# Storing the split halves of weight tiles in DRAM, in a two-layer hybrid trunk

## The chip, the cores and the metric

The kernel runs on one core of one Trainium2 chip. The metric is the device time of one execution in microseconds (us). A core has TensorE (PE in the profile; its weight loads are PEld), VectorE (DVE), ScalarE (ACT), GpSimd (POOL) and SyncE (SP), which here issues all DMAs between the chip's DRAM and the on-chip memory (SBUF). SyncE's queue is kept in order: an issue that waits for a semaphore holds up all issues behind it.

## What is computed

The reference is one inference step of a two-layer trunk: a prompt of 2048 rows of 1024 channels, and eight decode rows with states of their own. Each layer is

```python
hn = rms_norm(x, norm_w)
proj = hn @ w_in                    # 1024 x 3332
# split into four head groups, each with a mixer of its own:
#   A RetNet retention, H HGRN2 recurrence, S S5 state space + GLU, M Mamba-2 SSD
mixed = concatenate([o_ret, o_hgrn, o_s5, o_m2], axis=-1)
x = x + mixed @ w_out               # 1024 x 1024
```

The four mixers are recurrences along the prompt, and the states at its end are outputs too. A final RMSNorm ends the trunk.

## The kernel before

**Blocks and stages.** The prompt is cut into 4 blocks of 512 rows, so two layers make 8 blocks. A block has the input projections `gemm_A`, `gemm_H`, `gemm_S`, `gemm_M`, the mixers `mix_A` to `mix_M` and the output projection `out_proj`. A written order (`ORDER`) interleaves them: the S5 mixing of a block and its output projection run in the middle of the next block's phases. The decode rows ride along with the first block of each layer (`B.dec`).

**Split weights.** The products keep nearly full fp32 accuracy by splitting each operand into a high half, rounded to the fast type `float32r`, and the rest. A product is then three TensorE passes: low x high, high x low, high x high (`for pi, (a, c) in enumerate(((1, 0), (0, 1), (0, 0)))`). The activations are split once per block. The weights are loaded and split again for every block, tile by tile: SyncE loads 256 KB into a `wr` tile (`raw`), ScalarE casts it into the high half of a `wh` tile (`hl`; L606, L642), and VectorE subtracts that from the raw tile into the low half (L607, L643). The products of the decode rows use the raw tile, in the first block of a layer alone.

**Tiles.** `gemm_wide` takes 512 columns by 128 rows of the weight (L641 loads, L647 multiplies), `gemm` 256 columns by 2 x 128 rows (L603 loads, L605 the 4 tail columns of the time step; L622 and L590 multiply). A block has 68 tiles either way: 36 with `gemm` and 32 with `gemm_wide` in the first block of layer 0, 28 and 40 in the others, and in the last block the output projection goes by `gemm`, which makes 44 and 24.

**Buffers and order.** There are 7 buffers for `wr` (`NWR`) and 6 for `wh` (`NWH`). A `wr` buffer is free after the subtract (in a layer's first block, after the decode product); a `wh` buffer after the tile's last product on TensorE. The load, cast and subtract of a tile are traced with a raised priority (`WPRI` = 100); a planner orders each engine's instructions by priority and by its own idea of when operands and buffers are ready. [...]

**Other transfers.** The rows of a block are read twice (`xn`, 512 KB each: L526, L560), the residual in the output projection (L1538) is read and `xmid` written (L1543), and the S5 mixing reads seven constant tables of 512 KB (`big<-s5c`, L248). L1258 stores the S5 input into a tile of another layout, L752 writes decode rows, L1501 loads the final norm's weights.

Of the kernel before, what the change touches and what calls it, by code (L numbers as in the profile page):

```python
# [20 lines left out]
P = 128  # L21
D = 1024
KT = 8
# [93 lines left out]
def trunk_kernel(ctx: ExitStack, tc: tile.TileContext, A: dict):  # L117
# [31 lines left out]
    def nm(s):  # L149
        uid[0] += 1  # L150
        return f"{s}_{uid[0]}"
# [92 lines left out]
    s5c = [[drp.tile([P, 1024], F32, name=f"s5c{i}_{j}", tag=f"s5c{i}_{j}") for j in range(7)] for i in range(DEPTH)]  # L244

# [330 lines left out]
    def gemm(lhs, w, c0, mode, evac, dec=None, tail=None, ks=(0, 1, 2, 3), late=False):  # L576
# [55 lines left out]
    def gemm_wide(lhs, w, c0, evac, dec=None):  # L632
# [398 lines left out]
    def gemm_A(L, B):  # L1031
        w = A["w_in"][L.l]
# [14 lines left out]
        if B.l == 0 and B.b == 0:  # L1047
            qks = {}
            for part in range(2):
# [7 lines left out]
                gemm(B.hn, w, C_RQ + 256 * part, "T", ev1, dec=dec, late=part == 0)  # L1057
            B.qk = lambda tt, i: qks[i // 2, tt // 2][:, (tt % 2) * 256 + (i % 2) * P : (tt % 2) * 256 + (i % 2) * P + P]
        else:
# [7 lines left out]
            gemm_wide(B.hn, w, C_RQ, ev1, dec=dec)  # L1067
# [7 lines left out]
        gemm_wide(B.hn, w, C_RV, ev2, dec=B.dec and B.dec.chunk("rv"))  # L1075
# [53 lines left out]
    def gemm_H(L, B):  # L1129
        w = A["w_in"][L.l]  # L1130
# [11 lines left out]
        gemm(B.hn, w, C_GQ + 256, "F", ev1, dec=dec)  # L1142
        gemm(B.hn, w, C_GQ, "F", lambda m, ps: S.activation(B.gq[:, m, :], ps, AF.Silu), dec=dec)
# [7 lines left out]
        gemm_wide(B.hn, w, C_GI, ev2, dec=dec)  # L1151
# [98 lines left out]
    def gemm_S(L, B):  # L1250
        w = A["w_in"][L.l]
# [525 lines left out]
```

## Time and profile before

| | |
|---|---|
| time before | 2353.92 us, median of 3 runs (2349.15 to 2357.65) |
| span of the profiled execution | 2351.3 us |
| TensorE busy | 2186.8 us, 93% |
| VectorE busy | 1690.8 us, 72% |
| ScalarE busy | 1007.4 us, 43% |
| GpSimd busy | 247.0 us, 11% |
| DMA | 283.89 MB, mean 121 GB/s |
| mean granted clock of TensorE | 0.973 of full speed |

The profile is of one execution. Its span runs from the first to the last instruction; its time as a run was not listed apart from the three runs, and the span lies inside their spread. Busy shares are means over stages of different kind. TensorE's products are pipelined and their ends are modelled, so back-to-back products take less than their mean duration. Names such as `gb<-wh,hn` are the tile written and the tiles read; `wh` and `wr` are the split and raw weight tiles, `gb` the accumulators of the projections, `mb` those of everything else, `hn` and `mx` the split activations.

### The profile page before, as it was taken

Reading aid. Unit: us, or ns where it says so; the run is one execution under the profiler, and the core shown is the slowest. Engines: PE = TensorE matmul, PEld = TensorE weight load, DVE = VectorE, ACT = ScalarE, POOL = GpSimd, SP = SyncE. Lnnn points to the kernel's source line nnn. Section 1 sums busy time; section 2 is a strip of 40 time slices with the busy share of each in tenths; the row PEclk is TensorE's granted clock in tenths of the full one; section 3 lists DMA queues with packets and bytes.
Section 4 is the critical chain, followed back from the end, with each engine's and each line's share of the span. In section 5 each row is a group of like instructions: output and inputs, shape, how many; then the busy total and the mean of one; then the engine's idle time right before and its main releaser. Section 6 shows DMA issues by size and latency. Waiting matters only on the chain.

```text
span 2351.3 us, 41033 instructions
## 1 busy us (share of the span) xinstructions
PE 2186.8 (93%) x15047; PEld 1724.8 (73%) x15047; DVE 1690.8 (72%) x4625; ACT 1007.4 (43%) x1873; POOL 247.0 (11%) x212
## 2 busy tenths in 40 slices
PE   7997899999989999999899987999999999999897
PEld 6766676686767877788676775776877787777687
DVE  6778885578866687558856588855985568766686
ACT  5334545245442353424534245443454344443543
POOL 1020011001111011001110001100011001100100
PEclk9998899999999999999999998999999999999998
DMA  5334543433434644251333424526244352337222
GB/s 190 89 95 103 159 154 76 129 107 118 133 101 147 139 126 141 75 167 47 125 126 114 134 65 153 162 46 182 86 153 157 104 175 64 95 122 260 64 65 83
DMA packets 259226, 283.89 MB, mean 121 GB/s; under 512 B 88208, under 2 KB 184608, under 8 KB 259024
## 3 DMA queue, kind: packets, MB, share of 16 engines
q1 hardware_dynamic: 259024, 281.26, 39.8%
q8 instruction: 119, 1.95, 0.3%
q14 instruction: 83, 0.68, 0.1%
HBM read 245.00 MB, written 31.99 MB: 118 GB/s over the span
## 4 chain that ended last, share of the span: by engine, by line
PE 57%; DVE 20%; issue 6%; ACT 3%; DMA 2%; SPq 1%; POOL 1%; ACTq 0%; DVEq 0%; POOLq 0%
PE gb L647 25%; PE gb L622 10%; PE gb L590 5%; DVE big L1191 2%; PE mb L1332 1%; PE mb L1183 1%; DVE wh L643 1%; PE mb L569 1%; DMA big<-s5c 1%; DVE hHb L1240 1%; DVE half L1299 1%; PE gb L652 1%; PE mb L663 1%; SPq L940 1%; PE mb L1198 1%
## 5 line engine op out<-in xcount | busy, mean ns | idle before, releaser
L647 PE MATMUL gb<-wh,hn 128*128 128x512 f32 x2208 | 558.0, 402 | 4.9 <-DVE wh L643 4.3
L622 PE MATMUL gb<-hn,wh 128*128 128x512 f32 x1920 | 491.5, 403 | 0.1
L647 PEld LDWEIGHTS gb<-wh,hn 128*128 128x128 f32 x2208 | 408.1, 190 | 110.3 <-issue 13.5
L622 PEld LDWEIGHTS gb<-hn,wh 128*128 128x128 f32 x1920 | 348.9, 188 | 89.4 <-issue 8.8
L642 ACT CAST wh<-wr 128x512 fp32r<-128x512 f32 x296 | 182.7, 620 | 375.9 <-PE gb L647 184.5
L647 PE MATMUL gb<-wh,mx 128*128 128x512 f32 x1344 | 338.0, 402 | 0.0
L643 DVE TENSOR_TENSOR wh<-wr,wh 128x512 fp32r<-128x512 f32 x296 | 208.6, 712 | 170.5 <-ACT wh L642 169.6
L607 DVE TENSOR_TENSOR wh<-wr,wh 128x512 fp32r<-128x512 f32 (+1 forms) x248 | 176.9, 724 | 169.5 <-ACT wh L606 163.6
L647 PEld LDWEIGHTS gb<-wh,mx 128*128 128x128 f32 x1344 | 247.7, 189 | 63.5 <-issue 6.9
L606 ACT CAST wh<-wr 128x512 fp32r<-128x512 f32 (+1 forms) x248 | 151.6, 621 | 268.1 <-PE gb L647 103.8
L590 PE MATMUL gb<-wh,hn 128*128 128x256 f32 (+1 forms) x1728 | 233.3, 291 | 4.2 <-DVE hn L553 4.1
L590 PEld LDWEIGHTS gb<-wh,hn 128*128 128x128 f32 x1728 | 218.2, 194 | 13.3 <-DVE hn L553 5.9
L1445 POOL TENSOR_TENSOR half<-mats,m_lal 128x512 fp32r<-128x512 f32 x64 | 71.7, 1148 | 511.1 <-DVE m_lal L1423 301.6
L1183 PE MATMUL mb<-zb,big 128*64 128x64 f32 x1536 | 66.5, 242 | 38.8 <-ACT zb L1176 31.5
L1191 DVE COPY_PREDICATED big<-lvl,mb 64x256 f32<-64x256 int32 x192 | 93.0, 537 | 10.3 <-PE mb L1183 6.4
L1176 ACT COPY zb<-big 64x512 f32<-64x512 f32 x112 | 70.3, 628 | 64.0 <-DVE big L1204 54.2
L1183 PEld LDWEIGHTS mb<-zb,big 128*64 128x64 f32 x1536 | 56.6, 152 | 53.5 <-ACT zb L1176 38.2
L1166 POOL TENSOR_TENSOR big<-mats,h_dg 128x1024 f32<-128x1024 f32 x16 | 34.0, 2140 | 557.8 <-DVE h_dg L1163 438.5
L1367 DVE SCALAR_TENSOR_TENSOR big<-gb,vt,big 128x511 f32<-128x511 f32 (+2 forms) x96 | 66.9, 739 | 12.0 <-ACT big L1365 11.8
L671 ACT ACTIVATE half<-mb 128x512 f32<-128x512 f32 x32 | 19.1, 598 | 88.3 <-PE mb L1227 47.8
L1348 DVE TENSOR_TENSOR half<-half,big 128x512 f32<-128x512 f32 x16 | 10.9, 687 | 63.1 <-ACT half L1347 63.1
L1042 POOL TENSOR_TENSOR half<-half,half 128x256 f32<-128x256 f32 x32 | 27.2, 850 | 235.0 <-DVE half L1040 85.2
(493 smaller groups left out, 3240.7 us busy)
## 6 DMA issues: line engine op xcount, KB each, us to landing
wr<-in_w_in SPq DMA_DIRECT2D x416, 256.0 KB
wr<-in_w_out SPq DMA_DIRECT2D x128, 256.0 KB
big<-s5c SPq DMA_DIRECT2D x56, 512.0 KB
xn<-xmid SPq DMA_DIRECT2D x32, 512.0 KB
xn<-in_x_prompt SPq DMA_DIRECT2D x24, 512.0 KB
xmid<-half SPq DMA_DIRECT2D x44, 256.0 KB
half<-xmid SPq DMA_DIRECT2D x44, 256.0 KB
half<-in_x_prompt SPq DMA_DIRECT2D x32, 256.0 KB
```

The source lines that it names most:

```text
L590: T.matmul(out, lhs[2 * ks[ki] + k][:, a, tt * P : (tt + 1) * P], hls[ki][:, c, k, :n], start=(ki == 0 and k == 0 and pi == 0 and tt % per ...
L606: S.copy(hl[:, 0, :, :n], raw[:, :, :n])
L607: V.tensor_tensor(hl[:, 1, :, :n], raw[:, :, :n], hl[:, 0, :, :n].bitcast(F32), ALU.subtract)
L622: T.matmul(banks[i], hl[:, a, k, i * P : (i + 1) * P], lhs[2 * k2 + k][:, c, :], start=(ki == 0 and k == 0 and pi == 0), stop=(ki == 3 and ...
L642: S.copy(hl[:, 0, 0:512], raw[:, 0:512])
L643: V.tensor_tensor(hl[:, 1, 0:512], raw[:, 0:512], hl[:, 0, 0:512].bitcast(F32), ALU.subtract)
L647: T.matmul(banks[tt], lhs[kt][:, a, tt * P : (tt + 1) * P], hl[:, c, 0:512], start=(kt == 0 and pi == 0), stop=(kt == KT - 1 and pi == 2))
L1176: S.copy(qz[sl, r, :].rearrange("p (b h) -> p b h", h=h), q[sl].rearrange("p a (b two h) -> p (a b) two h", two=2, h=h)[:, :, 1, :])
L1183: T.matmul(ps[su, j * 64 : (j + 1) * 64], k[:, j // 4, (j % 4) * P + 64 * u : (j % 4) * P + 64 * u + 64], qz[:, :, j * 64 + 32 * u : j * 6 ...
L1191: V.copy_predicated(stv[p][su, :, nu * u : nu * u + nu, :], mv, ps[su, p * 256 : p * 256 + 256].rearrange("p (c b h) -> p c b h", c=8, h=h))
L1367: V.scalar_tensor_tensor(acc[:, 3 - i :], ps[:, : TB - 3 + i], w(i), acc[:, 3 - i :], ALU.mult, ALU.add)
L1445: E('m').tensor_tensor(mm.rearrange("p (h t) -> p h t", h=4), tri[:, None, :].to_broadcast([P, 4, P]), lal[:, i, tt, :][:, :, None].to_bro ...
```

## The change

The kernel gets a DRAM tensor `wsp` for each layer's `w_in` and `w_out`, with both halves of every element side by side by row. In the first block of a layer (`fresh`) tiles are loaded and split as before, and each split tile is also written to `wsp` by SyncE. In the other three blocks a tile's two halves are loaded straight into the `wh` tile, with no `wr` tile, cast or subtract. `gemm` does this in two DMAs of 256 KB per tile, one for each 128 rows (two more of 4 KB where there are tail columns), and `gemm_wide` in one DMA of 512 KB. Pieces stay 1 KB long in `gemm` and 2 KB in `gemm_wide`. Buffers, priorities and the written order are not touched. Every caller passes `fresh = B.b == 0` and the name of the weight in place of its array.

```diff
+    wsp = {(n, i): drp.tile([KT, P, 2, c], F32, name=f"ws_{n}{i}", tag=f"ws_{n}{i}")
+           for i in range(DEPTH) for n, c in (("w_in", PROJ), ("w_out", D))}
...
-    def gemm(lhs, w, c0, mode, evac, dec=None, tail=None, ks=(0, 1, 2, 3), late=False):
+    def gemm(lhs, wl, c0, mode, evac, dec=None, tail=None, ks=(0, 1, 2, 3), late=False, fresh=False):
+        w, ws = A[wl[0]][wl[1]], wsp[wl]
...
-                raw = wrp.tile([P, 2, 260], F32, name=nm("wr"), tag="wr")
-                rows = w[2 * k2 * P : 2 * (k2 + 1) * P].rearrange("(k p) c -> p k c", p=P)
-                nc.sync.dma_start(raw[:, :, 0:256], rows[:, :, c0 : c0 + 256])
-                if tail is not None:
-                    nc.sync.dma_start(raw[:, :, 256:260], rows[:, :, tail : tail + 4])
-                S.copy(hl[:, 0, :, :n], raw[:, :, :n])
-                V.tensor_tensor(hl[:, 1, :, :n], raw[:, :, :n], hl[:, 0, :, :n].bitcast(F32), ALU.subtract)
+                parts = [(0, 256, c0)] + ([(256, 260, tail)] if tail is not None else [])
+                raw = None
+                if fresh:
+                    raw = wrp.tile([P, 2, 260], F32, name=nm("wr"), tag="wr")
+                    rows = w[2 * k2 * P : 2 * (k2 + 1) * P].rearrange("(k p) c -> p k c", p=P)
+                    for a, b, c in parts:
+                        nc.sync.dma_start(raw[:, :, a:b], rows[:, :, c : c + b - a])
+                    S.copy(hl[:, 0, :, :n], raw[:, :, :n])
+                    V.tensor_tensor(hl[:, 1, :, :n], raw[:, :, :n], hl[:, 0, :, :n].bitcast(F32), ALU.subtract)
+                for k in range(2):
+                    for a, b, c in parts:
+                        d = ws[2 * k2 + k, :, :, c : c + b - a]
+                        if fresh:
+                            nc.sync.dma_start(d, hl[:, :, k, a:b].bitcast(F32))
+                        else:
+                            nc.sync.dma_start(hl[:, :, k, a:b].bitcast(F32), d)
...
-    def gemm_wide(lhs, w, c0, evac, dec=None):
+    def gemm_wide(lhs, wl, c0, evac, dec=None, fresh=False):
+        w, ws = A[wl[0]][wl[1]], wsp[wl]
...
-                raw = wrp.tile([P, 520], F32, name=nm("wr"), tag="wr")
-                nc.sync.dma_start(raw[:, 0:512], w[kt * P : (kt + 1) * P, c0 : c0 + 512])
-                S.copy(hl[:, 0, 0:512], raw[:, 0:512])
-                V.tensor_tensor(hl[:, 1, 0:512], raw[:, 0:512], hl[:, 0, 0:512].bitcast(F32), ALU.subtract)
+                raw = None
+                d = ws[kt, :, :, c0 : c0 + 512]
+                if fresh:
+                    raw = wrp.tile([P, 520], F32, name=nm("wr"), tag="wr")
+                    nc.sync.dma_start(raw[:, 0:512], w[kt * P : (kt + 1) * P, c0 : c0 + 512])
+                    S.copy(hl[:, 0, 0:512], raw[:, 0:512])
+                    V.tensor_tensor(hl[:, 1, 0:512], raw[:, 0:512], hl[:, 0, 0:512].bitcast(F32), ALU.subtract)
+                    nc.sync.dma_start(d, hl[:, :, 0:512].bitcast(F32))
+                else:
+                    nc.sync.dma_start(hl[:, :, 0:512].bitcast(F32), d)
...
-        w = A["w_in"][L.l]
+        w, fresh = ("w_in", L.l), B.b == 0
...
-                gemm_wide(B.mix, w, hf * 512, evac_wide(hf), dec=B.dec and B.dec.out(hf, last))
+                gemm_wide(B.mix, w, hf * 512, evac_wide(hf), dec=B.dec and B.dec.out(hf, last), fresh=fresh)
```

## Rows read from the trace of the kernel before

**Rows 1.** The page: span, busy time by engine, DMA queues.
```profile
span 2351.3 us, 41033 instructions
...
PE 2186.8 (93%) x15047; PEld 1724.8 (73%) x15047; DVE 1690.8 (72%) x4625; ACT 1007.4 (43%) x1873; POOL 247.0 (11%) x212
...
q1 hardware_dynamic: 259024, 281.26, 39.8%
```

**Rows 2.** Groups by line: busy us, mean ns | idle before, what ended it.
```profile
L647 PE MATMUL gb<-wh,hn 128*128 128x512 f32 x2208 | 558.0, 402 | 4.9 <-DVE wh L643 4.3 <-DVE rs L234 0.3
...
L643 DVE TENSOR_TENSOR wh<-wr,wh 128x512 fp32r<-128x512 f32 x296 | 208.6, 712 | 170.5 <-ACT wh L642 169.6
L642 ACT CAST wh<-wr 128x512 fp32r<-128x512 f32 x296 | 182.7, 620 | 375.9 <-PE gb L647 184.5 <-PE gb L622 59.6 <-DMA wr<-in_w_out 47.7
L607 DVE TENSOR_TENSOR wh<-wr,wh 128x512 fp32r<-128x512 f32 (+1 forms) x248 | 176.9, 724 | 169.5 <-ACT wh L606 163.6 <-DMA half<-xmid 2.1 <-DMA wr<-in_w_out 2.1
```

**Rows 3.** Chain of waits, 1600 to 1680 us: start, us, what.
```profile
1625.47 0.96 PE gb L652 x4
1626.43 5.74 PE gb L647 x24
...
1639.81 22.50 PE gb L622 x96
```

**Rows 4.** Waits of TensorE: us in total, times, longest.
```profile
PE mb L1183 <- ACT zb L1176: 31.5, 16, 5.4
```

**Rows 5.** Sum of the six stretches 294:590:870:1150 and 1450:1740:2020:2352 us: busy us.
```profile
sum 1758.00, PE 1664.28 PEld 1325.37 DVE 1250.44 ACT 760.67 POOL 183.90; mean PE 277.38 PEld 220.90 DVE 208.41 ACT 126.78 POOL 30.65
```

**Rows 6.** Chain by line: whole span, then 600 to 900, then 2020 to 2352 us.
```profile
by line: PE gb L647 25.3%; PE gb L622 9.7%; issue 5.9%; PE gb L590 5.0%; DVE big L1191 1.6%; PE mb L1332 1.4%; PE mb L1183 1.3%; DVE wh L643 1.3%; PE mb L569 1.2%; DMA big<-s5c 1.1%; DVE hHb L1240 1.0%; DVE half L1299 1.0%; PE gb L652 1.0%;
...
by line: PE gb L647 23.4%; issue 10.4%; PE gb L622 9.4%; PE gb L590 5.7%; DVE wh L643 2.4%; DMA big<-s5c 2.3%; DVE wh L607 1.9%; PE mb L1183 1.8%; DVE big L1191 1.6%; DVE hHb L1240 1.5%; DVE half L1299 1.3%; DVE rs L238 1.2%; DVE half L677 
...
by line: PE gb L647 21.2%; issue 12.8%; PE gb L590 10.0%; PE gb L622 7.9%; PE mb L1332 3.3%; PE mb L1345 2.2%; DVE half L1560 1.5%; PE mb L1183 1.3%; POOL half L1308 1.3%; DVE wh L607 1.2%; PE mb L663 1.2%; DVE half L1299 1.1%; DVE big L119
```

**Rows 7.** GEMM stretches, us: PE, PEld, DVE, ACT, POOL busy; clock, DMA share, GB/s.
```profile
35.00:130.00 95.00, 94.42 (x493) 68.83 (x488) 63.59 (x223) 38.49 (x76) 7.99 (x10) 1.00 0.40 118
440.00:475.00 35.00, 35.00 (x147) 23.25 (x144) 18.98 (x29) 11.61 (x19) 0.00 (x0) 1.00 0.64 201
...
755.00:803.00 48.00, 48.00 (x255) 41.04 (x254) 28.46 (x74) 17.10 (x30) 0.00 (x0) 1.00 0.80 182
1004.00:1072.00 68.00, 68.00 (x346) 57.41 (x344) 36.18 (x79) 21.98 (x39) 2.81 (x2) 1.00 0.50 146
1870.00:1938.00 68.00, 67.95 (x344) 57.44 (x345) 42.35 (x113) 27.43 (x54) 0.00 (x0) 1.00 0.59 177
```

**Rows 8.** Timeline at 437 us and of SyncE at 2047 us: start, us.
```profile
437.79 3.82 SPq L641 DMA_DIRECT2D wr<-in_w_out  x6
...
440.67 1.32 ACT L642 CAST wh<-wr 128x512 fp32r<-128x512 f32 x2 [12.87 <-DMA wr<-in_w_out]
...
2047.37 7.29 SPq L641 DMA_DIRECT2D wr<-in_w_out  x4
2054.70 8.32 SPq L248 DMA_DIRECT2D big<-s5c  x6
```

**Rows 9.** DMAs of 512 KB on the chain: start, us, what.
```profile
575.77 3.69 DMA xn<-in_x_prompt
...
632.18 6.92 DMA big<-s5c
```

**Rows 10.** Waits of SyncE's queue: us in total, times, longest.
```profile
SPq L641 <- DVE wh L643: 218.2, 78, 18.8
...
SPq L1258 <- ACT big L1256: 50.0, 6, 22.5
...
SPq L1543 <- DVE half L1539: 26.6, 23, 13.3
SPq L752 <- DVE half L992: 26.4, 2, 13.7
```

More of the change, by code (lines that the diff above doesn't have):

```diff
@@ L1055, in ev1 @@
                     qks[part, b2] = rotate(ps.rearrange("p t c -> p (t c)"), rt)
-                gemm(B.hn, w, C_RQ + 256 * part, "T", ev1, dec=dec, late=part == 0)
+                gemm(B.hn, w, C_RQ + 256 * part, "T", ev1, dec=dec, late=part == 0, fresh=fresh)
             B.qk = lambda tt, i: qks[i // 2, tt // 2][:, (tt % 2) * 256 + (i % 2) * P : (tt % 2) * 256 + (i % 2) * P + P]
@@ L1065, in ev1 @@
                 qkw[tt] = rotate(ps, rt)
-            gemm_wide(B.hn, w, C_RQ, ev1, dec=dec)
+            gemm_wide(B.hn, w, C_RQ, ev1, dec=dec, fresh=fresh)
             B.qk = lambda tt, i: qkw[tt][:, i * P : (i + 1) * P]
@@ L1073, in ev2 @@
             S.activation(B.rg[:, tt, :], ps[:, 256:512], AF.Silu)
-        gemm_wide(B.hn, w, C_RV, ev2, dec=B.dec and B.dec.chunk("rv"))
+        gemm_wide(B.hn, w, C_RV, ev2, dec=B.dec and B.dec.chunk("rv"), fresh=fresh)
     def mix_A(L, B):
@@ L1129, in gemm_H @@
     def gemm_H(L, B):
-        w = A["w_in"][L.l]
+        w, fresh = ("w_in", L.l), B.b == 0
         B.gq, B.gf, B.gk = big([P, 2, TB]), big([P, 2, TB]), big([P, 2, TB])
@@ L1141, in gemm_H @@
         dec = B.dec and B.dec.chunk("gf")
[L1142 to L1143 removed]
+        gemm(B.hn, w, C_GQ + 256, "F", ev1, dec=dec, fresh=fresh)
+        gemm(B.hn, w, C_GQ, "F", lambda m, ps: S.activation(B.gq[:, m, :], ps, AF.Silu), dec=dec, fresh=fresh)
         B.gi, B.gg = big([P, 4, 256]), big([P, 4, 256])
@@ L1149, in ev2 @@
             S.activation(B.gg[:, tt, :], ps[:, 256:512], AF.Silu)
-        gemm_wide(B.hn, w, C_GI, ev2, dec=dec)
+        gemm_wide(B.hn, w, C_GI, ev2, dec=dec, fresh=fresh)
     def mix_H(L, B):
@@ L1250, in gemm_S @@
     def gemm_S(L, B):
-        w = A["w_in"][L.l]
+        w, fresh = ("w_in", L.l), B.b == 0
         u = big([P, 4, 256])
@@ L1258, in ev1 @@
                 nc.sync.dma_start(B.U[32 * tt : 32 * tt + 32, :].rearrange("j (s c) -> j s c", s=4), u[:, tt, :])
-        gemm(B.hn, w, C_SU, "T", ev1, dec=B.dec and B.dec.chunk("su"))
+        gemm(B.hn, w, C_SU, "T", ev1, dec=B.dec and B.dec.chunk("su"), fresh=fresh)
         B.sg = big([P, 2, TB])
-        gemm(B.hn, w, C_SG, "F", lambda m, ps: S.activation(B.sg[:, m, :], ps, AF.Silu), dec=B.dec and B.dec.chunk("sg"))
+        gemm(B.hn, w, C_SG, "F", lambda m, ps: S.activation(B.sg[:, m, :], ps, AF.Silu), dec=B.dec and B.dec.chunk("sg"), fresh=fresh)
     def mix_S(L, B):
@@ L1356, in gemm_M @@
         nonlocal convc
-        w = A["w_in"][L.l]
+        w, fresh = ("w_in", L.l), B.b == 0
         xc = [big([P, 2, TB]), big([P, 2, TB])]
@@ L1373, in gemm_M @@
         dec = B.dec and B.dec.chunk("xbc")
-        gemm(B.hn, w, C_XBC, "F", ev1, dec=dec)
-        gemm(B.hn, w, C_XBC + 256, "F", lambda m, ps: ev1(m + 2, ps), dec=dec)
+        gemm(B.hn, w, C_XBC, "F", ev1, dec=dec, fresh=fresh)
+        gemm(B.hn, w, C_XBC + 256, "F", lambda m, ps: ev1(m + 2, ps), dec=dec, fresh=fresh)
         convc = cn
@@ L1383, in ev2 @@
             V.tensor_tensor(B.dtp[:, tt, :], ps[:, 256:260], L.dtb, ALU.add)
-        gemm(B.hn, w, C_MZ, "T", ev2, tail=C_DT, dec=B.dec and B.dec.chunk("mz"))
+        gemm(B.hn, w, C_MZ, "T", ev2, tail=C_DT, dec=B.dec and B.dec.chunk("mz"), fresh=fresh)
     def softplus(out, x, shape, tag):
@@ L1495, in out_proj @@
     def out_proj(L, B, src, dst, last):
-        w = A["w_out"][L.l]
+        w, fresh = ("w_out", L.l), B.b == 0
         fwb = [None, None]
@@ L1571, in out_proj @@
                     dec = B.dec and B.dec.out(hf // 2, last)
-                gemm(B.mix, w, hf * 256, "T", evac(hf), dec=dec, ks=KS_LAST, late=hf == 3)
+                gemm(B.mix, w, hf * 256, "T", evac(hf), dec=dec, ks=KS_LAST, late=hf == 3, fresh=fresh)
         if dbg is not None:
```

## The prediction

> **What bounds the kernel now.** I read the page first [rows 1]. TensorE is busy 93% of a 2351.3 us span, VectorE 72%, ScalarE 43%, and the 16 DMA engines 39.8% for 121 GB/s. So look for what TensorE does and what it waits for. The groups by line [rows 2] show the work that the change touches: 296 + 248 = 544 VectorE subtracts of 712 and 724 ns (L643 and L607), and before each a ScalarE cast of 620 ns (L642; L606 is alike). They also show that the casts mostly wait for TensorE ("PE gb L647" ended 184.5 us of the idle before L642): a weight tile is split as soon as a `wh` buffer comes free, long before it is used, and TensorE itself waited for a split only 4.3 us (L647). The chain of waits [rows 3] shows how a pure GEMM stretch runs: 96 products of 512 columns in 22.50 us. A weight tile feeds 12 of them (or 24 of half the columns), so it lasts 2.8 us, and nothing of the split shows there. In those stretches the change can only lose.
>
> What is left is the mixing, where TensorE's small products wait for VectorE and ScalarE: the longest in total [rows 4] is L1183's for a ScalarE copy, 31.5 us. There a subtract or cast that stands in the engine's queue ahead of the awaited operation delays TensorE. The sum over the stretches of the six blocks that will load halves [rows 5] bounds this: 1758 us, in which TensorE is busy 1664.3, so idle 94 us in all.
>
> **The change, part by part.** Each block has 68 weight tiles. Layer 0's first block splits 36 with `gemm` and 32 with `gemm_wide`, layer 1's first 28 and 40, so 64 and 72 splits stay and 184 + 224 = 408 go.
>
> *Removed splits.* ScalarE loses 408 x 0.62 = 253 us. VectorE loses 224 x 0.712 + 184 x 0.724 = 293 us of 1691. As most of both is off the path, I price it by what of it stands on the chain [rows 6]. L643 is 1.3% of the span there, 30.6 us; by count 224/296 of it goes, 23 us. L607 is under the page's 1%, but in the stretch 600 to 900 us it is 1.9% of 300 us, 5.7 us, and in the last block 1.2% of 332 us, 4.0 us. Together 33 us, which I take as the gain. Bounds: nothing, if a second chain of nearly the same length takes over each time; 94 us, if every TensorE idle in the loading blocks went.
>
> *Loads of twice the size.* 408 loads bring 512 KB, not 256 KB: 107 MB more. In a GEMM stretch that is 256 KB more per 2.8 us, 94 GB/s. The stretches without a fresh split [rows 7] have 146 GB/s at a DMA share of 0.50 (1004 to 1072 us) and 177 at 0.59 (1870 to 1938), so a full share is worth 290 to 300 GB/s. They rise to shares of 0.82 and 0.91. The stretch 755 to 803 us, which also carries the small transfers of the next layer's setup, is at 0.80 and would be full. The work that hides this is the tiles already in `wh`: six buffers, one in use, five ahead, 5 x 2.8 = 14 us. A load is landed and cast 2.9 us after its issue in the timeline [rows 8], and a 512 KB load on the chain took 3.7 to 6.9 us [rows 9]; both fit in 14 us. Without that cover each tile would cost TensorE about 4 us. Price for the weights: nothing.
>
> *What is behind them.* All DMAs go out from SyncE's one queue. A weight load that waits for a buffer holds up what is queued behind it: at 2047 us four loads took 7.3 us and the `s5c` loads of the S5 mixing followed [rows 8]. That stays as it is, since in both kernels TensorE's pace sets when the buffer is free. But those `s5c` loads are on the chain [rows 9], and each now shares the DMA engines with one 256 KB more per weight tile ahead of it, 0.8 us at 300 GB/s. One per block makes 8 x 0.8 = 6 us. Bounds: 0 and 20 us (three tiles ahead of it).
>
> *Stores of the fresh tiles.* 136 tiles x 512 KB = 71 MB written, 72 stores for the wide tiles and 128 for the others, with 16 small ones for the tail columns. Each waits in SyncE's queue for its subtract; loads and stores behind it wait too. The nearest row is the store of `xmid` behind its VectorE add: 26.6 us in 23 waits [rows 10], 1.2 us each, so 200 stores that all wait so long make 240 us. SyncE already stands 218 us for the raw buffers after L643 alone [rows 10], and up to five split tiles, 14 us, lie ahead of TensorE, so I price this wait at nothing, with an upper bound of 15 us for the first blocks, where one wait in that row was 13.3 us. The extra issues (216 stores, 208 second loads, at 0.6 us as in the six of 3.82 us [rows 8]) make 270 us of SyncE's time that go into its waits for buffers; without these they would come on top.
>
> The bytes cost more. In the two output projections of first blocks a tile lasts 3.4 us (24 products of 5.7 us and decode products of 0.96 us for two tiles [rows 3]), so 16 tiles are 54 us. In the first of them the DMA engines are at 0.64 with 201 GB/s [rows 7], 314 GB/s when full. Each tile adds 512 KB of store, 8.4 MB, 27 us of all engines; with the present work, 0.64 x 54 = 35 us, that is 62 us in a stage of 54, 8 us over. The seven `wr` and six `wh` buffers absorb some: I take 5 us each, 10 us (bounds 0 and 16). The first block's input projections go from 0.40 [rows 7] to about 0.9 (a tile per 3.4 us adds 154 GB/s): 2 us for each layer, 4 us (bounds 0 and 20).
>
> The Trainium skill, "DMA: Bandwidth & Descriptors", section "Where 436 GB/s comes from", puts the limit of transfers with HBM at about 358 GB/s per core. By it the output stages, which ask for about 360, would just fit, and the sum, called an estimate, would be 10 us lower. The rows give 290 to 314 for this kernel's 1 and 2 KB pieces, and I go by them.
>
> *Sum.* -33 + 6 + 10 + 4 = -13 us: a span of 2338. The median of the runs, 2353.9 us, is 2.6 us over this execution's span, so **2341 us**, 0.6% faster. About 0.3% is what a measurement can tell from no change.
>
> **The rivals.**
>
> *Full relief* (15%). VectorE's queue gets a sixth shorter overall and a quarter shorter in the loading blocks, so that waits shorten beyond the operations on the chain. For it: the waits of rows 4. Against: TensorE is busy 95% of these blocks. Two thirds of the 94 us less 20 us of costs gives 43 us: 2311 us.
>
> *No effect* (19%). The chain moves to TensorE or to other VectorE work of the same length, and the removed 33 us shrink to the 20 us that the transfers cost: 2354 us. For it: splits are done far ahead of use.
>
> *The DMA engines become the bound, slower* (22%). Mean traffic goes from 284 MB to 462 MB, about 65% of the engines' span, unevenly: the fresh stages are over 1, and every GEMM stretch at 0.8 to 0.9. It decides from where a stretch asks for more than 14 us of backlog. Then 8 us over in each output stage, 10 us in each first block, and a backlog that spills over about 3 us in the six loading blocks: 16 + 20 + 18 = 54 us, less a gain of 25: 2383 us. Against it: the cover of 14 us. The Trainium skill, same page, section "Queues, rings and completion order", says that an engine consumes a queue's descriptors in ring order. By that rule small urgent loads stand behind the bulk; the `s5c` load of rows 9 agrees as far as it takes 6.9 us, against 3.7 for another of the same size.
>
> *Half the prefetch, slower* (13%). Before, 7 raw and 6 split tiles were ahead, 36 us of GEMM; the loading blocks have 6. Every stall of SyncE's queue over about 10 us then reaches TensorE. Waits of 22.5, 13.7 and 13.3 us on other things exist [rows 10]. If half a dozen of them cost 8 us each and the gain is 25 us: 2354 + 23 = 2377 us.
>
> That the change does not do what it says could be, if a load waited for stores of other columns. Those are a whole phase older, so this has no price.
>
> **How the numbers follow.** My forecast has 31%, its own range 2325 to 2347. With full relief that makes 46% for faster, 19% for the same, 22 + 13 = 35% for slower. The range of 8 in 10 reaches from 2303 (most of the 94 us gained) to 2388 (all upper bounds of the transfers with a small gain).
>
> **What would show it.** Right: casts and subtracts at 64 and 72; VectorE near 1400 us busy and ScalarE near 755; DMA share near 0.65; in pure GEMM stretches still 2.8 us per tile, with TensorE waiting nowhere on `wh` loads; less of L1183's wait; `s5c` pieces on the chain near 8 us. Wrong: TensorE waiting for DMAs of the stored halves, a GEMM stretch slower than 2.9 us per tile, or more than 4 us per tile in the first blocks' projections. The largest unknown is the order of all engines' work, which is laid out anew when 816 instructions go; no row shows it.

## The result and the profile after

The changed kernel takes 2377.66 us (median of 4 runs, 2371.69 to 2386.04) against 2352.61 us for the kernel before: ratio 1.0112, 95% interval 1.0086 to 1.0139. It is slower by 1.1%, about 26 us; 2341 us, faster, was forecast. The profiled execution is the longest of the four, 2386.04 us, with a span of 2384.3 us, 33.0 us longer than that of [rows 1].

The page of the changed kernel, the lines that answer to [rows 1]:

```profile
span 2384.3 us, 40291 instructions
...
PE 2203.6 (92%) x15047; PEld 1739.8 (73%) x15047; DVE 1436.2 (60%) x4217; ACT 776.9 (33%) x1468; POOL 223.4 (9%) x212
...
q1 hardware_dynamic: 403024, 459.71, 62.7%
```

The engines' work moved about as forecast: VectorE lost 255 us of work and ScalarE 230 us (293 and 253 were forecast), and the DMA engines went from 39.8% to 62.7%. TensorE, which does the same 15047 products, is busy 17 us longer. Part of the lost time is therefore products that run longer: a mean of 406 ns in place of 402 in the first row below [rows 2], at a mean granted clock of 0.962 in place of 0.973. The same groups by line (busy us, mean ns | idle before, what ended it):

```profile
L667 PE MATMUL gb<-wh,hn 128*128 128x512 f32 x2208 | 565.2, 406 | 11.6 <-DMA wh<-ws_w_in 6.6
...
L659 ACT CAST wh<-wr 128x512 fp32r<-128x512 f32 x72 | 44.6, 620 | 161.9 <-PE gb L667 71.8
L660 DVE TENSOR_TENSOR wh<-wr,wh 128x512 fp32r<-128x512 f32 x72 | 50.1, 705 | 78.3 <-ACT wh L659 78.0
```

Where did the time go? Cut each span at the first product of each block's HGRN mixing (L1161 before, L1181 after), and compare stretch by stretch. The columns are length, busy time of PE, PEld, DVE, ACT and POOL with their instructions, granted clock, DMA share, GB/s. The kernel before:

```profile
0.00:197.00 197.00, 174.94 (x1084) 132.35 (x1084) 144.94 (x508) 81.86 (x171) 26.70 (x36) 0.97 0.40 122
197.00:508.00 311.00, 282.21 (x1915) 217.67 (x1912) 222.53 (x595) 130.48 (x236) 27.51 (x21) 0.95 0.46 128
508.00:803.00 295.00, 273.58 (x1811) 219.10 (x1811) 219.74 (x651) 120.56 (x219) 36.77 (x33) 0.96 0.45 127
803.00:1071.00 268.00, 256.94 (x1754) 206.74 (x1753) 180.79 (x454) 116.22 (x209) 26.28 (x23) 0.99 0.39 119
1071.00:1365.00 294.00, 280.05 (x1902) 209.67 (x1900) 206.04 (x511) 121.97 (x224) 29.02 (x24) 0.99 0.35 110
1365.00:1674.00 309.00, 282.72 (x1920) 217.51 (x1916) 229.80 (x626) 136.12 (x254) 27.10 (x21) 0.96 0.41 124
```

The changed kernel:

```profile
0.00:207.00 207.00, 177.95 (x1084) 134.02 (x1084) 147.52 (x510) 85.73 (x174) 24.09 (x36) 0.95 0.74 227
207.00:527.00 320.00, 286.75 (x1917) 219.36 (x1910) 192.52 (x545) 102.05 (x186) 25.88 (x21) 0.94 0.67 197
527.00:820.00 293.00, 271.61 (x1817) 218.92 (x1816) 180.44 (x586) 81.37 (x151) 34.96 (x33) 0.97 0.63 189
820.00:1087.00 267.00, 257.75 (x1753) 209.04 (x1752) 132.74 (x385) 76.16 (x140) 24.10 (x23) 0.98 0.64 193
1087.00:1388.00 301.00, 282.74 (x1897) 215.11 (x1899) 192.97 (x491) 111.09 (x205) 25.52 (x24) 0.97 0.62 199
1388.00:1708.00 320.00, 288.98 (x1920) 219.76 (x1913) 201.27 (x588) 108.26 (x204) 24.43 (x21) 0.94 0.62 192
```

The loss sits in four stretches: the first (+10 us), the second (+9) and, in layer 1, the fifth (+7) and sixth (+11). The first and the fifth hold the storing block's projections, the second and the sixth its later stages and the start of the block that loads first. The pure loading stretches 527 to 820 and 820 to 1087 us lost 87 us of VectorE's work between them and became 2 and 1 us shorter. These are lengths of the longest of four executions; by the medians the whole loss is 26 us, not 33. Two questions need experiments: why the work removed bought nearly nothing, and what costs some 10 us at each of these places.

TensorE's waits in the changed kernel (us in total, times, longest):

```profile
PE mb L1203 <- DVE big L1225: 20.8, 10, 3.4
...
PE mb L981 <- DVE half L974: 10.5, 2, 5.8
...
PE mb L1304 <- DMA big<-s5c: 7.2, 6, 4.2
...
PE gb L667 <- DMA wh<-ws_w_in: 6.6, 7, 1.6
...
PE gb L594 <- DMA wh<-ws_w_in: 2.7, 2, 2.5
```

The wait of [rows 4], L1183 for a ScalarE copy, is no longer among the longest; the same line now waits for VectorE. L981 is new near the top of this list: the first product of the decode rows' S5 step, two waits, one in each layer, 10.5 us where the kernel before has 2.2 (its L961). The waits for `s5c`, the urgent transfer for which the forecast added 6 us, rose from 1.4 us (L1284 before) to 7.2. Those for stored weights are 6.6 + 2.7 = 9.3 us. The pace of a pure GEMM stretch is also what it was in [rows 3], 24 products in 5.7 us, by the chain of waits:

```profile
1650.35 5.72 PE gb L667 x24
```

### The profile page after: what moved, and what is told of

Read it like the earlier page. It is cut to its first block, busy times and chain, and to the rows that moved or that the text cites. A ratio compares the mean times of both kernels' runs of the same rounds, so it can differ in the third digit from the quotient of the medians.

```text
span 2384.3 us, 40291 instructions
## 1 busy us (share of the span) xinstructions
PE 2203.6 (92%) x15047; PEld 1739.8 (73%) x15047; DVE 1436.2 (60%) x4217; ACT 776.9 (33%) x1468; POOL 223.4 (9%) x212
## 3 DMA queue, kind: packets, MB, share of 16 engines
q1 hardware_dynamic: 403024, 459.71, 62.7%
## 5 line engine op out<-in xcount | busy, mean ns | idle before, releaser
L667 PE MATMUL gb<-wh,hn 128*128 128x512 f32 x2208 | 565.2, 406 | 11.6 <-DMA wh<-ws_w_in 6.6
L635 PE MATMUL gb<-hn,wh 128*128 128x512 f32 x1920 | 500.5, 408 | 0.0
L667 PEld LDWEIGHTS gb<-wh,hn 128*128 128x128 f32 x2208 | 413.7, 192 | 117.6 <-issue 16.7
L594 PE MATMUL gb<-wh,hn 128*128 128x256 f32 (+1 forms) x1728 | 240.0, 295 | 8.4 <-DVE wh L613 3.0
L594 PEld LDWEIGHTS gb<-wh,hn 128*128 128x128 f32 x1728 | 222.1, 197 | 18.4 <-DVE hn L556 4.1
L1559 DVE TENSOR_TENSOR half<-half,gb 128x512 f32<-128x512 f32 x56 | 37.7, 685 | 103.5 <-PE gb L667 91.8
L659 ACT CAST wh<-wr 128x512 fp32r<-128x512 f32 x72 | 44.6, 620 | 161.9 <-PE gb L667 71.8
L660 DVE TENSOR_TENSOR wh<-wr,wh 128x512 fp32r<-128x512 f32 x72 | 50.1, 705 | 78.3 <-ACT wh L659 78.0
L613 DVE TENSOR_TENSOR wh<-wr,wh 128x512 fp32r<-128x512 f32 (+1 forms) x64 | 44.3, 705 | 32.4 <-ACT wh L612 32.1
L612 ACT CAST wh<-wr 128x512 fp32r<-128x512 f32 (+1 forms) x64 | 39.1, 620 | 75.4 <-DMA wr<-in_w_in 37.3
L685 ACT ACTIVATE mx<-mb,vt 128x512 fp32r<-128x512 f32 x48 | 31.2, 686 | 90.4 <-PE gb L667 69.1
```

The source lines that it names most:

```text
L594: T.matmul(out, lhs[2 * ks[ki] + k][:, a, tt * P : (tt + 1) * P], hls[ki][:, c, k, :n], start=(ki == 0 and k == 0 and pi == 0 and tt % per ...
L635: T.matmul(banks[i], hl[:, a, k, i * P : (i + 1) * P], lhs[2 * k2 + k][:, c, :], start=(ki == 0 and k == 0 and pi == 0), stop=(ki == 3 and ...
L667: T.matmul(banks[tt], lhs[kt][:, a, tt * P : (tt + 1) * P], hl[:, c, 0:512], start=(kt == 0 and pi == 0), stop=(kt == KT - 1 and pi == 2))
```

## The experiments

Times are medians; ratios are to the kernel before, run beside it on the same chip, with the 95% interval. 1% is 23.5 us. The profile's time of one execution can lie several us from the median, so sizes are taken from the ratios, and places from the traces.

**First question: the two halves of the change apart.** `loads_only` keeps the loads and drops the stores:

```
+    wz = drp.tile([P, 2, PROJ], F32, ...)     # one tile in DRAM, written once
-                d = ws[kt, :, :, c0 : c0 + 512]
+                d = wz[:, :, 0:512]
-                    nc.sync.dma_start(d, hl[:, :, 0:512].bitcast(F32))
+                    if not stored:
+                        stored.append(1)
+                        nc.sync.dma_start(d, hl[:, :, 0:512].bitcast(F32))
```

(and alike in `gemm`). Expected: 

> This kernel has the changed kernel's 512 KB loads in three of four blocks and no stores of fresh tiles: every load reads the one split tile that is stored once, so its later blocks compute with the wrong weights; sizes, pieces, queues and buffers of the loads are those of the changed kernel. Theory 1 (the first blocks pay for the stores, the loading blocks neither gain nor lose much): 2340 to 2356 us, no longer than before, and the first blocks' segments as long as before. Rival (the loads of twice the size, with six tiles of prefetch, cost it): 2365 us or more, with the loading blocks longer than before.

Measured: 2365.16 us, 1.0057 (1.0041 to 1.0074).

`half_loads` is the same with a single load of 256 KB per tile into the high half, which the products use for the low half too:

```
-                    nc.sync.dma_start(hl[:, :, 0:512].bitcast(F32), d)
+                    nc.sync.dma_start(hl[:, 0, 0:512].bitcast(F32), d[:, 0, :])
```

Expected: 

> No stores of fresh tiles but one, and in the later blocks a tile is one load of 256 KB into the high half, which stands in for the low half too (its products lack the low half, and the weights are those of one tile): so neither splits nor extra bytes. It shows what the removal of 408 casts and subtracts is worth by itself. By the prediction's term: 33 us less than before, 2320 us, or less with full relief. Rival (TensorE sets the pace in the loading blocks, and VectorE's and ScalarE's work there was hidden): 2343 to 2354 us.

Measured: 2339.24 us, 0.9944 (0.9925 to 0.9962). This is the price of the 408 splits with no more bytes moved than before: 13 us, not 33. It is a net sum: some stretches became longer, such as that from block 0's to block 1's HGRN mixing, 315.4 us in this trace and 311.1 before.

`stores_only` lets every block split and the first blocks also store:

```
-                if fresh:
+                if True:
                     raw = wrp.tile([P, 520], F32, name=nm("wr"), tag="wr")
...
-                    nc.sync.dma_start(d, hl[:, :, 0:512].bitcast(F32))
-                else:
-                    nc.sync.dma_start(hl[:, :, 0:512].bitcast(F32), d)
+                    if fresh:
+                        nc.sync.dma_start(d, hl[:, :, 0:512].bitcast(F32))
```

Expected: 

> All eight blocks split their tiles as before; the first block of a layer also stores its halves (71 MB), and nobody reads them. Theory 1 (stores cost the first blocks some 35 us): 2380 to 2392 us. Rival (the loads cost it): 2352 to 2360 us.

Measured: 2369.48 us, 1.0076 (1.006 to 1.0092). `stores_tiny` keeps each of these stores, but of 4 columns:

```
-                        nc.sync.dma_start(d, hl[:, :, 0:512].bitcast(F32))
+                        nc.sync.dma_start(d[:, :, 0:4], hl[:, :, 0:4].bitcast(F32))
```

Expected: 

> As the kernel with stores alone, but each store carries 4 columns of its tile and not 256 or 512: the same number of stores in SyncE's queue, behind the same subtracts, with about 1% of the bytes. If the price of the stores is their bytes on the DMA engines: 2352 to 2360 us. If it is their waits in SyncE's queue and the longer hold of the split buffers: 2372 to 2390 us.

Measured: 2354.25 us, 1.0009 (0.9996 to 1.0022). All issues and all waits for the split are still there and cost nothing that can be told from zero; the bytes cost the 16 us that are left.

The parts together: -13 (splits), +27 (loads of twice the size, `half_loads` to `loads_only`) and +18 (stores) make some +31 us, against +26 for the whole change. The ratios behind these numbers are known to 4 to 6 us each, so the parts and the whole agree within what can be told.

**Second question: where the doubled loads cost 27 us.** Take the same product in `half_loads` and in `loads_only` and compare its start in both traces. Up to 388 us the two run within 3 us of each other, and 15 us later `loads_only` is 11 us behind. The largest other step, 8 us, comes at the same place of layer 1; one of 5 us, at about 660 us, stands where TensorE waits 3.2 us for a weight tile (1.1 us in `half_loads`). The timeline of TensorE in `loads_only` there (start, us, what, [idle before and its end]):

```profile
385.61 3.92 PE L669 MATMUL gb<-wh,hn 128*128 128x512 f32 x15
395.61 0.23 PE L983 MATMUL mb<-ct,half 64*8 64x16 f32 x4 [6.08 <-DVE half L976]
395.77 2.50 PE L669 MATMUL gb<-wh,hn 128*128 128x512 f32 x5
```

and the stretch cut around it, with the columns of the tables above:

```profile
370.00:389.00 19.00, 18.21 (x112) 13.06 (x109) 5.38 (x13) 11.46 (x15) 0.00 (x0) 1.00 0.65 154
389.00:395.00 6.00, 0.54 (x3) 0.10 (x1) 3.34 (x3) 0.00 (x0) 0.00 (x0) 0.87 0.11 11
395.00:405.00 10.00, 9.39 (x79) 5.88 (x80) 2.96 (x9) 0.00 (x0) 0.00 (x0) 0.50 0.18 53
```

TensorE stands for 6 us at the decode rows' S5 step of block 0, with block 1's products queued behind. The granted clock then is 0.50, the 1.2 GHz level, for some 10 us, which costs about another 5 (an estimate: half of that time). Nothing of this is a wait for weights. VectorE in turn waited for its input:

```profile
DVE big L967 <- DMA big<-pd_su: 3.9, 1, 3.9
```

That input, `ub`, comes in 16 small transfers on SyncE's queue (L960 in the changed kernel, L940 before). SyncE's timeline in the kernel before:

```profile
367.42 8.91 SPq L940 DMA_DIRECT2D big<-pd_su  x13
...
377.69 1.96 SPq L940 DMA_DIRECT2D big<-pd_su  x3
```

and in the changed kernel:

```profile
370.17 5.74 SPq L663 DMA_DIRECT2D wh<-ws_w_in  x4
379.11 1.97 SPq L960 DMA_DIRECT2D big<-pd_su  x3
382.25 0.54 SPq L663 DMA_DIRECT2D wh<-ws_w_in  x1
382.84 4.85 SPq L960 DMA_DIRECT2D big<-pd_su  x7
...
389.52 0.56 SPq L663 DMA_DIRECT2D wh<-ws_w_in  x1
390.12 5.94 SPq L960 DMA_DIRECT2D big<-pd_su  x6
```

Before, 13 of the 16 go out without a gap, and all within 12.2 us. After, weight loads stand between them; they take 17.0 us, and the last six take 5.94 us in place of 6 x 0.63, since a single issue lasted up to 2.57 us. The chain has no slack even before (TensorE waits 2.2 us at its end, over both layers), so a later `ub` is a longer TensorE wait.

Not all of the longer wait is the transfers'. The place of this step in TensorE's order differs too. Here is the time up to its first product, with TensorE's products counted, in the kernel before, in the changed kernel, and in `after_ub2`, which follows below:

```profile
0.00:388.35 388.35, 337.77 (x2270) 260.34 (x2270) 298.22 (x934) 171.68 (x338) 50.98 (x56) 0.95 0.46 129
...
0.00:402.68 402.68, 340.67 (x2259) 260.82 (x2259) 281.76 (x903) 157.82 (x309) 46.40 (x56) 0.93 0.71 212
...
0.00:399.65 399.65, 344.48 (x2272) 263.27 (x2272) 282.76 (x905) 157.87 (x309) 46.62 (x56) 0.93 0.71 214
```

In the changed kernel, and in `loads_only` (2259 as well), 11 products of block 1's projections stand behind the step that stood ahead of it before. At 24 products in 5.72 us they are 2.6 us of the 5.8 us wait (an estimate). The planner lays the order out anew for every kernel, so the kernels below change the transfers and this place together. They show what is lost at this step, and not how much of it is the late input and how much the earlier place. Four kernels test whether the loss is at this step.

`loads_late` is `loads_only` with halves loaded in blocks 2 and 3 of a layer only, the condition changed in five lines:

```
-        w, fresh = ("w_in", L.l), B.b == 0
+        w, fresh = ("w_in", L.l), B.b <= 1
```

Expected: 

> The first two blocks of each layer split as before the change, only the last two load the doubled tiles (512 KB, all from one stored tile, so the numbers in the product are not the weights' own); nothing but one tile is stored. Theory: the doubled loads cost where small urgent transfers of the layer's first block and its decode rows are still under way behind them, in the stretch from block 0's HGRN mixing to block 1's (326 us with loads only, 311 before) and the same stretch of layer 1 (317 against 309); blocks 2 and 3 lose nothing by them and keep the gain of the missing splits. Then 2340 to 2350 us, and those two stretches are back within 3 us of 311 and 309. Rival, the doubled loads cost the same in every block: two thirds of the 13 us that loads only lost against the kernel before, 2357 to 2363 us.

Measured: 2350.0 us, 0.9981 (0.9972 to 0.9991). The stretch 199 to 511 us is 312.4 us long, as against 326.1 in `loads_only`, and TensorE's waits for the chain are 2.2 us in two places, as in the kernel before (10.9 us in `loads_only`). A third of the loads cost more than the other two thirds together: taking them out gives back 18 us, although 136 splits return.

`loads_noub` leaves block 1's loads as they are in `loads_only` and does not fetch `ub`:

```
-                for b in range(8):
-                    nc.sync.dma_start(ub[64 * r : 64 * r + 64, b], uv[r, b].partition_broadcast(64))
+            V.memset(ub, 0.5)
```

Expected: 

> Loads only (2365 us), with the decode rows' S5 input of each layer not fetched at all: the tile is set to 0.5 by VectorE, so those decode outputs are not the reference's. Theory: both waits for that chain go, 2340 to 2350 us, as with loads late (2350) or below. Rival, the next transfer behind the bulk takes the wait's place, or the loss is spread: 2356 us and more.

Measured: 2343.48 us, 0.9957 (0.9944 to 0.997), within 4 us of `half_loads`, with all the doubled loads in place. So up to 23 of their 27 us are lost at this one step; its own transfers are left out with it, which is worth a few us by itself (next).

`after_ub2` is the changed kernel with that input in 2 transfers a layer, same bytes, 14 issues fewer:

```
-                for b in range(8):
-                    nc.sync.dma_start(ub[64 * r : 64 * r + 64, b], uv[r, b].partition_broadcast(64))
+                nc.sync.dma_start(ub[64 * r : 64 * r + 64], uv[r].partition_broadcast(64))
```

Expected: 

> The changed kernel with one edit: the decode rows' S5 step fetches its input, spread over 128 partitions, by 2 transfers a layer in place of 16 (the same bytes), so SyncE's queue issues 14 fewer of 0.63 us each in the place where TensorE waited 5 us for VectorE and ran at the lower clock behind it, in each layer. Theory, the doubled loads cost through this one chain (11 and 10 us of the 16 between loads late and loads only): 2352 to 2362 us in place of 2378. Rival, the wait lies with the bytes in front of and within this transfer and not with its issues: 2372 to 2380 us. Rival, the doubled loads wear on every block: 2370 us and more.

Measured: 2364.02 us, 1.0045 (1.0028 to 1.0061): 16 us gained by the ratios, and L981's wait is gone from the trace. `before_ub2`, the control, has the same edit on the kernel before. Expected: 

> The kernel before with the same edit of the decode rows' S5 step, the control: its TensorE waited only 2 us there in all, so under the theory 2348 to 2354 us, no or hardly any change. If it gains as much as the changed kernel does from the edit, the chain is not what the doubled loads cost.

Measured: 2349.47 us, 0.9983 (0.9972 to 0.9994): 4 us. The changed kernel gains four times as much, as it must if this step is where the loads cost. So some 12 us of the loss are shown to be here by an edit that leaves out no work. In the traces the two stretches that hold the step became 8.2 and 11.4 us shorter, and 1.5 and 2.8 us in the control.

**Rivals on the loads.** `half_loads_2x` fetches each narrow tile in two transfers of 128 KB:

```
-                        nc.sync.dma_start(hl[:, 0, :, a:b].bitcast(F32), wz[:, :, 0 : b - a])
+                        for k in range(2):
+                            nc.sync.dma_start(hl[:, 0, k, a:b].bitcast(F32), wz[:, k, 0 : b - a])
```

Expected: 

> As the run with loads of half the size (2339 us; the high half stands for the low one too), but each tile of the narrow products is fetched by two transfers of 128 KB in place of one of 256 KB, as many issues as in the changed kernel at half its bytes. Theory, bytes are what costs: 2337 to 2343 us. Rival, the number of transfers and of waits in SyncE's queue costs: 2355 us and more, most of the way to loads only (2365).

Measured: 2333.88 us, 0.9915 (0.9899 to 0.9931), below the expected range: more issues of the weights cost nothing. The 7 us gained by the ratios are at the edge of what can be told, as the two intervals overlap. `before_two_loads` tried this on a kernel with all its work (the kernel before, `ub` in 2 transfers, raw narrow tiles in two):

```
-                nc.sync.dma_start(raw[:, :, 0:256], rows[:, :, c0 : c0 + 256])
+                for k in range(2):
+                    nc.sync.dma_start(raw[:, k, 0:256], rows[:, k, c0 : c0 + 256])
```

Expected: 

> The kernel before with the decode rows' S5 input by 2 transfers in place of 16 (2349 us) and each raw tile of the narrow products fetched by two transfers of 128 KB in place of one of 256 KB. With loads of half the size the second edit gave 5 us (2339 to 2334). If that came of the smaller transfers: 2341 to 2346 us. If it came of how the program happened to be ordered: 2346 to 2354 us, either way.

Measured: 2349.34 us, 0.9984 (0.9974 to 0.9994), the same as `before_ub2`. The gain doesn't carry over.

`loads_wh8_wr3` is `loads_only` with other numbers of tiles:

```
-NWR = 7
-NWH = 6
+NWR = 3
+NWH = 8
```

Expected: 

> As loads only (2365 us, the loads of the changed kernel without its stores, all from one stored tile), with eight tiles for split weights and three for raw ones in place of six and seven. Theory of small transfers that wait behind bulk: more bulk is issued ahead, so no help, 2360 to 2370 us. Rival, the six tiles are too few to hide the doubled loads: 2340 to 2350 us, near the run with loads of half the size (2339).

Measured: 2412.79 us, 1.0248 (1.0231 to 1.0265), outside both. Three raw tiles starve the first blocks, which split as before: the stretch to block 0's HGRN mixing is 228.9 us, 197.2 in `loads_only`. The stretch that matters (block 0's to block 1's HGRN mixing) is 324.6 us against 326.1, so two more tiles ahead did not help there; the next one is 285 against 293. It tells little, because two things were changed.

**The stores.** `stores_half` stores only the low half of each tile, in as many transfers:

```
-                        nc.sync.dma_start(d, hl[:, :, 0:512].bitcast(F32))
+                        nc.sync.dma_start(d[:, 1], hl[:, 1, 0:512].bitcast(F32))
```

Expected: 

> Stores only (2369 us), with only the low half of each tile stored, so half the bytes in the same number of transfers. If the stores cost by their bytes in proportion: midway between 4 columns a store (2354) and both halves, 2359 to 2365 us. If they cost only from the point at which the first blocks' transfers no longer fit: 2352 to 2357 us.

Measured: 2366.15 us, 1.0047 (1.0035 to 1.0059); midway between 1.0009 and 1.0076 is 1.0043. By the medians that is in proportion to bytes. The trace does not bear it out. Of the 13.7 us by which its span exceeds that of the kernel before, 9 lie in the stretch between the HGRN mixing of blocks 1 and 2 of layer 1, which has no store in it. The kernel before and `stores_half`:

```profile
1673.70:1937.70 264.00, 256.40 (x1758) 207.60 (x1756) 186.64 (x501) 121.40 (x225) 28.68 (x21) 0.99 0.44 135
...
1679.40:1952.40 273.00, 260.09 (x1758) 211.60 (x1756) 188.00 (x503) 122.48 (x226) 29.75 (x21) 0.97 0.43 131
```

The four stretches that do hold stores are 1116 us long in `stores_half`, 1117 in `stores_tiny` and 1129 in `stores_only`. By place, then, half the bytes cost nothing more than tiny stores, and a threshold is not excluded. These are single executions, so this stays open.

One place is plain in `stores_only`. The kernel before in its first 140 us:

```profile
0.00:100.00 100.00, 85.02 (x490) 65.73 (x491) 66.98 (x260) 49.05 (x107) 10.54 (x23) 0.98 0.49 150
100.00:140.00 40.00, 40.00 (x200) 28.57 (x199) 28.97 (x107) 14.32 (x30) 7.86 (x7) 1.00 0.39 116
```

`stores_only`:

```profile
0.00:100.00 100.00, 85.36 (x493) 66.67 (x494) 60.46 (x226) 45.98 (x98) 10.15 (x23) 0.98 0.84 265
100.00:140.00 40.00, 36.47 (x155) 25.64 (x154) 29.66 (x126) 18.59 (x37) 2.99 (x4) 0.91 0.76 238
```

and the waits of TensorE from 100 to 210 us, the longest in the kernel before and two in `stores_only`:

```profile
PE mb L849 <- DVE half L847: 6.0, 1, 6.0
...
PE mb L866 <- DVE convc L1385: 6.8, 1, 6.8
PE mb L461 <- DMA half<-in_s_C_re: 3.3, 2, 2.2
```

In the first 100 us TensorE does as much as before, at a DMA share of 0.84. Then it waits for a constant of the S5 setup (`s_C_re`), not for weights, and the mean granted clock falls from 1.00 to 0.91. The wait of 6.8 us is no cost of the stores: the same line (L849 before) waits 6.0 us without them.

`stores_pool` issues the stores from GpSimd:

```
-                            nc.sync.dma_start(d, hl[:, :, k, a:b].bitcast(F32))
+                            nc.gpsimd.dma_start(d, hl[:, :, k, a:b].bitcast(F32))
```

Expected: 

> Stores only (2369 us: every block splits, the first blocks also store both halves), with the stores issued from GpSimd's queue in place of SyncE's. If the stores cost because the loads behind them in SyncE's queue wait for their bytes: 2352 to 2360 us, near the run with 4 columns a store (2354). If the bytes take the 16 DMA engines' time wherever they are issued: 2365 to 2375 us. If issuing them holds up GpSimd's own work (4 us waits of VectorE and TensorE for it): above 2375 us.

Measured: 2385.93 us, 1.0141 (1.0127 to 1.0155). The bytes did not become cheaper on another queue: in the first 100 us the DMA share is 0.83 below, 0.84 with SyncE's. The Trainium skill ("DMA: Bandwidth & Descriptors", section "Issuing engines are not separate DMA queues") says that transfers run on the same 16 DMA engines whichever engine starts them; these rows agree. How much of the further loss is GpSimd's own is not separated; it is busy four times as long in the first 100 us:

```profile
0.00:100.00 100.00, 83.05 (x477) 64.22 (x478) 62.65 (x238) 46.63 (x102) 39.78 (x64) 0.97 0.83 275
```

`late_halves` is the whole change one block later: blocks 0 and 1 split, block 1 stores, blocks 2 and 3 load:

```
-                    nc.sync.dma_start(d, hl[:, :, 0:512].bitcast(F32))
+                    if dec is None:     # block 0 has the decode rows
+                        nc.sync.dma_start(d, hl[:, :, 0:512].bitcast(F32))
...
-        w, fresh = ("w_in", L.l), B.b == 0
+        w, fresh = ("w_in", L.l), B.b <= 1
```

Expected: 

> The changed kernel with everything one block later: blocks 0 and 1 of a layer split, block 1 stores the halves, blocks 2 and 3 load them. Theory: the stores (18 us when they stood alone in block 0) lie in a block without decode rows and cost less, the loads cost nothing in blocks 2 and 3, and two thirds of the gain of the missing splits (8 us of 12) stays: 2342 to 2358 us. Rival, bytes cost the same wherever they move: stores 18, loads two thirds of 26, less 8 for the splits, so 2375 to 2382 us.

Measured: 2375.99 us, 1.0091 (1.0077 to 1.0105). The theory failed here, and the time is in the rival's range: the stores cost 26 us on top of `loads_late`, more than in block 0. (One more execution of the same kernel, on record as `late_halves_ub2` although it has no `ub` edit, took 2378.16 us.) Its trace shows why in part: the wait of L983 for the decode chain, 2.2 us in `loads_late`, is back with 8.2 us, as eight of block 1's stores are issued in the 8 us ahead of the first `ub` transfer of layer 0. `late_halves_16to2` adds the `ub` edit. Expected: 

> The changed kernel one block later (2376 us: blocks 0 and 1 of a layer split, block 1 stores, blocks 2 and 3 load), with the decode rows' S5 input fetched by 2 transfers in place of 16. TensorE waited 8 us for that chain there in its profile, with the lower clock behind it, and not at all with the same loads and no stores (loads late). If the stores cost through that chain: 2355 to 2365 us. If they cost by their bytes in the block itself: 2369 us and more.

Measured: 2366.19 us, 1.006 (1.0046 to 1.0074), between the two ranges: 7 us by the ratios, of which the control has 4. So the rest of the price is not that chain's, and moving the stores does not save them.

**Is any part of the change worth keeping?** `wout_16to2` has it in the output projections alone, with the `ub` edit; `w_in` is split every time and not stored:

```
-        w, fresh = ("w_in", L.l), B.b == 0
+        w, fresh = ("w_in", L.l), 2
...
-                    nc.sync.dma_start(d, hl[:, :, 0:512].bitcast(F32))
+                    if fresh is True:
+                        nc.sync.dma_start(d, hl[:, :, 0:512].bitcast(F32))
```

Expected: 

> The kernel before with the change in the output projections alone (their first block of a layer stores 16 tiles, the later blocks load them; all input projections split every time and store nothing), and the decode rows' S5 input by 2 transfers in place of 16. The kernel before with the latter edit alone took 2349 us. By the prices so far (18 us for 136 stored tiles, 12 us for 408 missing splits, nothing for these loads, which are not ahead of the decode chain): plus 4, minus 3, so 2346 to 2354 us. If the output projections are where the splits cost most: 2335 to 2343 us.

Measured: 2351.07 us, 0.9994 (0.9986 to 1.0003), no better than `before_ub2`. No version with stored halves beat the kernel before by a measurable amount; the fastest complete kernel is the kernel before with the decode rows' input in 2 transfers, 0.2% below it.

## Why the prediction was wrong

Two terms of its sum failed, both by about 20 us, and both against the change.

*"Price for the weights: nothing", and 6 us for "what is behind them".* Measured: 27 us. The first half of the step held: TensorE waits for stored weights 9.3 us in all, and the GEMM pace is unchanged. The second half failed. It took the `s5c` loads for the only urgent transfers behind the bulk, as they "are on the chain", and said of the weight loads that hold up SyncE's queue: "That stays as it is". The transfers that cost most, the 16 of `ub`, were on the chain of the kernel before as well. The chain by line on its page names them last but one (`SPq L940`), and the chain from 350 to 400 us goes through one issue after the other to the landing of the last:

```profile
PE gb L647 25%; PE gb L622 10%; PE gb L590 5%; DVE big L1191 2%; PE mb L1332 1%; PE mb L1183 1%; DVE wh L643 1%; PE mb L569 1%; DMA big<-s5c 1%; DVE hHb L1240 1%; DVE half L1299 1%; PE gb L652 1%; PE mb L663 1%; SPq L940 1%; PE mb L1198 1%
...
368.13 0.63 SPq L940
...
379.02 2.37 DMA big<-pd_su
```

The issues of L940 are 9.4 us of this chain, and there is a second such piece of 9.9 us in layer 1. Of the whole span the two are 0.8%, less than any line shown in [rows 6], whose two other stretches leave out both places. Nor did the queue stay as it was: weight loads went out between these issues where none did before. The question not asked was which small transfers share SyncE's queue with the bulk, and how many us each could be late. The 6 us for `s5c` came out in number only. Its waits rose by 5.8 us, but `half_loads`, which moves no more bytes than the kernel before, has 7.4 us of them, so the shared bytes are not the reason.

The ring order of the Trainium skill ("DMA: Bandwidth & Descriptors", section "Queues, rings and completion order"), which the prediction used for a rival, is at most a small part of this. The last `ub` transfer landed 2.4 us after its issue before the change (379.0 to 381.4 us), and VectorE's operation on it began 3.3 us after that issue in the changed kernel (395.4 to 398.7). So the data behind the bulk came less than 1 us later, while the 16 issues took 4.7 us longer.

*"I take -33", the splits on the chain.* Measured: -13 (`half_loads`). The step counted every subtract on the chain at its full length. When they go, another operation takes over. The waits of TensorE in `half_loads` on the line of [rows 4]:

```profile
PE mb L1206 <- DVE big L1228: 16.8, 10, 3.4
...
PE mb L1206 <- ACT zb L1199: 8.4, 8, 1.7
```

The wait for ScalarE fell by 23 us, from 31.5 us, and the wait of the same line for VectorE rose from 7.2 us to 16.8. This was the bound "nothing, if a second chain of nearly the same length takes over"; the truth lay between the bounds, nearer that one. `wout_16to2` fits: it leaves the input projections' splits, and its wait for ScalarE stays at 29.9 us.

*The stores.* 14 us forecast, 18 measured, and the waits in SyncE's queue at nothing (`stores_tiny`): about right in size. The place was another: the larger part was put into the output projections, which were to run over their time, while in the first block the trace shows late setup constants. In the changed kernel the wide products of the output projections wait 0.4 us in all, 0.2 of it for a split. So the size is in part luck. Here are the stretches that answer to the second and third of [rows 7]:

```profile
455.00:490.00 35.00, 35.00 (x150) 22.88 (x150) 12.74 (x21) 7.54 (x12) 0.00 (x0) 1.00 0.81 266
772.00:820.00 48.00, 48.00 (x256) 40.98 (x255) 17.84 (x59) 7.36 (x13) 0.00 (x0) 1.00 0.93 242
```

The first is an output projection that stores; even at a DMA share of 0.93, in the second, TensorE is busy throughout.

*The rivals.* Two slower ones gave 2383 and 2377 us, beside the 2378 measured, by mechanisms that did not decide. "The DMA engines become the bound" wanted 18 us spread over the loading blocks, 8 us over in each output stage and GEMM stretches that slow down: there are none. Its 10 us in each first block come near the first and fifth stretch (10 and 7 us longer), where the forecast had 2 each; but with tiny stores the first stretch is already 5.7 us longer. "Half the prefetch" wanted long waits for `wh`: 9.3 us in all, the longest 2.5. The clean test of that rival, more split tiles with seven raw ones, was not made.

What stays open: how much of the loss at the decode rows' S5 step is the late input and how much the step's earlier place in TensorE's order; what the store bytes cost and where, with the engines' mean share at 0.48 in `stores_only`; why `late_halves` pays more for them than block 0; and whether the narrow loads in two pieces gained anything in `half_loads`. A new order of the work may itself shift a stretch by some us, and could be behind the 9 us in a stretch without stores; no run holds the order fixed.

## What to carry to other kernels

Doubling a bulk stream that is itself well prefetched can still cost: list the small transfers that share its issuing queue, and for each the slack until an in-order engine needs it. Read the chain of waits stretch by stretch: a row of short issues, together under 1% of the span, can be on it and have no slack. Look at the order of the products too, where a planner lays it out anew for every change. Price removed work by what takes its place on the engine that waits, not by its own length on the chain. And when a small transfer is in the way, fewer issues of it (16 to 2 here) may give more than any change of the bulk.

## What was unexpected of the hardware

In `loads_only` a 6 us stand of TensorE at 389 us was followed by 10 us at a granted clock of 0.50, so that it cost nearly twice its length; in the changed kernel, after a 5.8 us stand at the same place, the clock over the next 11 us was 0.86. The issue of a small transfer on SyncE, 0.63 us as a rule, took up to 1.29 us in the kernel before and up to 2.57 us in the changed one. And 71 MB of stores cost 15 us more from GpSimd's queue than from SyncE's.
